# Retention in a two-layer trunk: the states of both directions in one 128-row stack

## The chip, the core and the metric

The kernel runs on one core of a Trainium2 chip. The metric is the device time of one execution in microseconds (us), as the median of several runs. The engines are TensorE (PE; its weight loads are listed apart as PEld), VectorE (DVE), ScalarE (ACT), GpSimd (POOL) and SyncE (SP, which issues the DMA transfers). Each engine works through its own list of instructions in a fixed order, and waits on semaphores for the others.

## What is computed

Two layers of a trunk over 256 context and 512 latent tokens, width 1024. Each layer projects its input to three groups of heads (a Mamba-2 SSD, a latent attention called MLA, and retention), gates each, and projects their concatenation back. The retention group has 4 heads with keys and queries of 64 and values of 128 channels, and runs a scan with a constant decay per head, once forward and once backward, in chunks of 128 tokens:

```python
def chunked_scan(q, k, v, log_a, h0):
    """h_t = exp(log_a_t) h_{t-1} + k_t v_t^T ;  y_t = q_t . h_t   (chunkwise form)"""
    ...
    y_intra = jnp.einsum('bcijgh,bcjghp->bcighp', scores[..., None] * decay, vc)
    to_end = jnp.exp(cum[:, :, -1:] - cum)
    states = jnp.einsum('bcjgn,bcjghp->bcghnp', kc, vc * to_end[..., None])
    chunk_decay = jnp.exp(cum[:, :, -1])
    ...                                   # h_in: chunk_decay * h + s, carried from chunk to chunk
    y_inter = jnp.einsum('bcign,bcghnp->bcighp', qc, h_in) * jnp.exp(cum)[..., None]

def retention_mixer(p_c, p_l, log_rate_f, log_rate_b, cos, sin, with_ctx):
    ...
    for log_rate, rev in ((log_rate_f, False), (log_rate_b, True)):
        ...
        yc, yl = directional_scan(qc, kc, vc, ..., ql, kl, vl, ..., rev)
    y_l = head_norm(ys_l[0] + ys_l[1]) ; out_l = y_l * silu(gate_l)
```

There are six chunks: 0 and 1 are context, 2 to 5 latent. The forward scan visits 0 1 2 3 4 5, the backward one 1 0 5 4 3 2. Layer 0 needs outputs for all six chunks, layer 1 only for the latent four.

## The kernel before

The tokens lie along the free dimension and channels on the 128 partitions. The program is written stage by stage, and a scheduler then sets the order of instructions on each engine from priorities and from its own idea of when things are ready; `high_priority` blocks (line 153 and others) pull work forward. So work of neighbouring stages is mixed: projections of the gate z (`zstage`, PSUM tile `pj`, names `zt`, `zy`, `yg`) run between the pieces of retention, and later ones, or products with the output weights (`po`), between those of MLA. Each 128x1024 weight tile is loaded (`wr`), cast on ScalarE (`wh`) and its remainder taken on VectorE (`wl`) before use. Projections use three products of rounded halves; retention uses float32 products, which the profile shows as two records each.

`ret` (line 730) first makes the decay tables: `Dm` for pairs of tokens inside a chunk, `ef` for queries, `te` for keys, `cd` for the carry of one chunk. It loads and rotates queries `q` and keys `kk`, two heads of 64 rows to a tile of 128 partitions. Line 781 transposes each chunk's keys on TensorE to a PSUM tile `pkt`, and line 782 copies it to `kt`. `state` (line 784) is called ten times a layer, five for each direction: VectorE multiplies `kt` by `te` to `kd`, four products with the values `rvt`, 64 columns wide, fill `prst`, and the carry (line 799, tile `rh`) adds the decayed state before. `ret_y` (line 816) is called for each pair of chunks, three times in layer 0 and twice in layer 1: scores `prs` (line 827, 64 rows each), their decayed form `mt` (tag `rmt`), decayed queries `qe` (tag `rqe`), and then line 848, for each of 4 heads and 2 chunks, one product of `rvt` with `rmt` (128 rows) and one for each direction that has an incoming state, of `rh` with `rqe` (64 rows), all into `pry`. The rest of it squares, sums (`prc`), takes the inverse root (`rs_y`, `rs_t`), spreads it (`prb`) and multiplies with the gate `rgt`.

Of the kernel before, what the change touches and what calls it, by code (L numbers as in the profile page):

```python
# [9 lines left out]
F32 = mybir.dt.float32  # L10
# [3 lines left out]
AF = mybir.ActivationFunctionType  # L14
ALU = mybir.AluOpType
# [8 lines left out]
NCH = T // 128  # L24
# [68 lines left out]
class Trunk:  # L93
# [636 lines left out]
    def ret(self, P):  # L730
        nc, l, D, ctx, lo = self.nc, self.l, self.D, self.ctx, self.lo
        pc, K = self.pc[l], self.K
        k = lambda a: K[:, a:a + 128]

        lamp = P.tile([128, 4], F32, name="lamp")
        self.act(lamp, pc[:, P_RF:P_RF + 4], AF.Exp)
        self.ts(lamp, lamp, -1.0, ALU.mult)
        lamr = P.tile([128, 8], F32, name="lamr")
        self.act(lamr, pc[:, P_RR:P_RR + 8], AF.Exp)
        self.ts(lamr, lamr, -1.0, ALU.mult)  # L740
        Dm = P.tile([128, 4, 128], F32, name="Dm")
        for h in range(4):
            self.ts(Dm[:, h], k(C_R1), lamr[:, h:h + 1], ALU.mult)
            self.stt(Dm[:, h], k(C_R2), lamr[:, 4 + h:5 + h], Dm[:, h], ALU.mult, ALU.add)
        self.act(Dm, Dm, AF.Exp)
        self.tt(Dm, Dm, k(C_OD).unsqueeze(1).to_broadcast([128, 4, 128]), ALU.mult)
        ef = P.tile([128, 2, 2, 128], F32, name="ef")
        for d in range(2):
            for p in range(2):
                self.act(ef[:, d, p], k(C_PF if d == 0 else C_PB), AF.Exp, scale=lamp[:, d * 2 + p:d * 2 + p + 1])  # L750
        cd = P.tile([128, 4], F32, name="cd")
        self.act(cd, lamp, AF.Exp, scale=128.0)
        te = P.tile([128, 2, 4], F32, name="te")
        for d in range(2):
            self.act(te[:, d], lamr[:, 4 * d:4 * d + 4], AF.Exp, scale=K[:, C_PE + d:C_PE + d + 1])
        self.ts(te, te, 0.125, ALU.mult)
        rt = P.tile([128, 2, NLAT], F32, tag="rmt", name="rt", bufs=1)
        rc, rs = rt[:, 0], rt[:, 1]
        self.load(rt, self.A["rope"][0:2].rearrange("s p t -> p s t"))

        q, kk = [], []
        for nm, src, dst, full in (("rq", D["rq"], q, ctx), ("rk", D["rk"], kk, True)):
            for t in range(2):
                u = P.tile([128, T], F32, name=f"{nm}{t}")
                a0 = 0 if full else NCTX
                self.load(u[:, a0:], src[t][:, a0:])
                w = P.tile([128, NLAT], F32, tag="rsw", name="rsw", bufs=2)
                for b in range(4):
                    self.load(w[32 * b:32 * b + 32, :], src[t][32 * (b ^ 1):32 * (b ^ 1) + 32, NCTX:T])
                self.tt(u[:, NCTX:T], u[:, NCTX:T], rc, ALU.mult)  # L770
                self.tt(w, w, rs, ALU.mult)
                self.tt(u[:, NCTX:T], u[:, NCTX:T], w, ALU.add)
                dst.append(u)
        v = P.tile([128, NCH, 512], F32, name="rvt")
        self.load(v, D["rv"])

        kt = P.tile([128, NCH, 256], F32, name="kt")
        for c in range(NCH):
            p = self.ps("py", "pkt", 2)
            for t in range(2):  # L780
                nc.tensor.transpose(p[:, t * 128:(t + 1) * 128], kk[t][:, c * 128:(c + 1) * 128], self.ident)
            self.copy(kt[:, c], p[:, 0:256])

        def state(c, d, h):
            p = self.ps("ps", "prst", 2)
            kd = P.tile([128, 4, 64], F32, tag="kd", name="kd", bufs=2)
            self.tt(kd, kt[:, c].rearrange("p (h e) -> p h e", e=64), te[:, d].unsqueeze(2).to_broadcast([128, 4, 64]),
                    ALU.mult)
            for hd in range(4):
                pr, s = divmod(hd, 2)  # L790
                self.mm(p[64 * s:64 * s + 64, pr * 128:(pr + 1) * 128], kd[:, hd, :],
                        v[:, c, hd * 128:(hd + 1) * 128])
            hn = P.tile([128, 2, 128], F32, tag=f"rh{d}", name="rh", bufs=5 if d else 3)
            pv = p[:, 0:256].rearrange("p (a e) -> p a e", e=128)
            if h is None:
                self.copy(hn, pv)
            else:
                for pr in range(2):
                    self.stt(hn[:, pr], h[:, pr], cd[:, d * 2 + pr:d * 2 + pr + 1], pv[:, pr], ALU.mult, ALU.add)
            return hn  # L800

        hs = ({}, {})
        h = None
        for c in (1, 0, 5, 4, 3, 2):
            hs[1][c] = h
            if c != 2:
                h = state(c, 1, h)
        h = None
        for c in range(NCH):
            hs[0][c] = h  # L810
            if c != NCH - 1:
                h = state(c, 0, h)
            if c % 2 == 1 and c - 1 in self.chunks:
                self.ret_y(P, c - 1, q, kk, v, Dm, ef, hs)

    def ret_y(self, P, c0, q, kk, v, Dm, ef, hs):

        nc, D = self.nc, self.D
        cs = slice(c0 * 128, (c0 + 2) * 128)
        v3 = lambda t: t.rearrange("p (a c i) -> p a c i", a=2, c=2)  # L820
        ps = [self.ps("ps", "prs", 2) for _ in range(2)]
        for h in range(4):
            pr, s = divmod(h, 2)
            r = slice(64 * s, 64 * s + 64)
            for cc in range(2):
                c1 = slice((c0 + cc) * 128, (c0 + cc + 1) * 128)
                self.mm(v3(ps[s])[:, pr, cc], kk[pr][r, c1], q[pr][r, c1])
        mt = P.tile([128, 2, 2, 2, 128], F32, tag="rmt", name="rmt", bufs=1)
        for s in range(2):
            self.tt(mt[:, s], v3(ps[s]), Dm.rearrange("p (a s) i -> p a s i", s=2)[:, :, s].unsqueeze(2)  # L830
                    .to_broadcast([128, 2, 2, 128]), ALU.mult)
        qe = P.tile([128, 2, 2, 2, 128], F32, tag="rqe", name="rqe", bufs=1)
        for d in range(2):
            for pr in range(2):
                self.tt(qe[:, d, pr], q[pr][:, cs].rearrange("p (c i) -> p c i", i=128),
                        ef[:, d, pr].unsqueeze(1).to_broadcast([128, 2, 128]), ALU.mult)
        py = [self.ps("py", "pry", 2) for _ in range(2)]
        for h in range(4):
            pr, s = divmod(h, 2)
            r = slice(64 * s, 64 * s + 64)  # L840
            for cc in range(2):
                c = c0 + cc
                ops = [(v[:, c, h * 128:(h + 1) * 128], mt[:, s, pr, cc])]
                for d in range(2):
                    if hs[d][c] is not None:
                        ops.append((hs[d][c][r, pr, :], qe[r, d, pr, cc]))
                for i, (a, b) in enumerate(ops):
                    self.mm(v3(py[s])[:, pr, cc], a, b, i == 0, i == len(ops) - 1)

        sq = P.tile([128, 2, 512], F32, tag="rmt", name="rsq", bufs=1)  # L850
        gt = P.tile([128, 2, 2, 256], F32, tag="rgt", name="rgt", bufs=1)
        pcl = self.ps("pb", "prc", 1)
        for s in range(2):
            self.act(sq[:, s], py[s], AF.Square)
            for j in range(4):
                self.mm(pcl[:, s * 4 + j:s * 4 + j + 1], sq[:, s, j * 128:(j + 1) * 128], self.ones[:, 0:1])
            for pr in range(2):
                self.load(gt[:, s, pr], D["rg"][pr * 2 + s][:, cs])
            gf = gt[:, s].rearrange("p a i -> p (a i)")
            self.tt(gf, py[s], gf, ALU.mult)  # L860
        var = P.tile([128, 8], F32, tag="rvar", name="rvar", bufs=2)
        self.ts(var, pcl[:, 0:8], 4.0 / 128, ALU.mult, 4.0 * LN_EPS, ALU.add)
        rstd = self.rsqrt(P, var, 8)
        for s in range(2):
            pb = self.ps("pb", "prb", 1)
            for j in range(4):
                self.mm(pb[:, j * 128:(j + 1) * 128], rstd[:, s * 4 + j:s * 4 + j + 1].to_broadcast([128, 128]),
                        self.ident)
            gf = gt[:, s].rearrange("p a i -> p (a i)")
            self.tt(gf, gf, pb, ALU.mult)  # L870
            for pr in range(2):
                self.load(D["m"][4 + pr * 2 + s][:, cs], gt[:, s, pr])
# [478 lines left out]
```

## Time and profile before

| what | value |
|---|---|
| three runs, us | 1536.39, 1538.78, 1549.31 (median 1538.78) |
| the profiled execution | 1534.29 us, span 1532.5 us |
| mean granted TensorE clock | 0.979 |
| TensorE, VectorE, ScalarE, GpSimd busy | 96%, 71%, 46%, 3% of the span |
| retention of layer 0, of layer 1 | about 407 to 475 us and 1183 to 1242 us after the start |

The span runs from the first to the last instruction. Busy time is the time in which an engine works on at least one instruction; a TensorE product overlaps with the next one, so the starts of products tell what each occupies better than their durations. The chain of waits goes back from the last instruction through whatever released each step; its pieces do not overlap and add up to time. A clock of 1.00 is 2.4 GHz, 0.50 is 1.2 GHz.

### The profile page before, as it was taken

To read this page: it belongs to the slowest core of one execution; us is meant where nothing else is said; L and a number is where in the kernel's file an instruction comes from. 1 tells how busy PE (TensorE), PEld (TensorE's weight loads), DVE (VectorE), ACT (ScalarE), POOL (GpSimd) and SP (SyncE) were. 2 spreads that over 40 slices of the span, in tenths; PEclk is the share of its full clock that TensorE was granted. 3 is DMA by queue.
4 is the path that set the end of the run, shared out by engine and by line. 5 is a ranking of instruction groups with operands and counts; after the bars stand their busy time and mean duration, and the time that the engine had idled before them with its cause. 6 is when DMAs were issued, how large, how long until landed. Compare 5 with 4: busy or idle time off the path is not lost. (4 is left out here: it accounts for less than half of the span.)

```text
span 1532.5 us, 24217 instructions
## 1 busy us (share of the span) xinstructions
PE 1465.7 (96%) x9044; PEld 1181.1 (77%) x9044; DVE 1085.8 (71%) x2117; ACT 709.3 (46%) x1414; POOL 48.5 (3%) x43
## 2 busy tenths in 40 slices
PE   6999999999999998999999899999999999999995
PEld 4787789778878777777788778788778777767785
DVE  3599995974544566777645978997785456888867
ACT  2356654762211434477622434565463134457743
POOL 0000000000000000000003140000000000000010
PEclk9999999999998999999999899999999999999998
DMA  8335653667614845543343233343357266544253
GB/s 330 128 112 168 196 168 115 179 203 232 206 63 131 270 150 157 165 123 126 104 143 113 99 140 106 117 138 118 99 175 250 70 193 216 144 153 122 85 178 110
DMA packets 114190, 233.52 MB, mean 152 GB/s; under 512 B 14028, under 2 KB 45644, under 8 KB 113816
## 3 DMA queue, kind: packets, MB, share of 16 engines
q1 hardware_dynamic: 114072, 231.97, 47.7%
q8 instruction: 71, 1.16, 0.3%
q14 instruction: 47, 0.39, 0.1%
HBM read 181.73 MB, written 50.20 MB: 151 GB/s over the span
## 5 line engine op out<-in xcount | busy, mean ns | idle before, releaser
L105 PE MATMUL pj<-hh,wh 128*128 128x512 f32 (+2 forms) x984 | 357.4, 364 | 2.0 <-ACT hh L119 1.6
L105 PE MATMUL pj<-hh,wl 128*128 128x512 f32 (+1 forms) x984 | 356.2, 362 | 0.0
L105 PE MATMUL pj<-hl,wh 128*128 128x512 f32 (+1 forms) x984 | 352.1, 358 | 0.0
L126 ACT CAST wh<-wr 128x1024 fp32r<-128x1024 f32 (+1 forms) x132 | 137.1, 1040 | 235.2 <-PE pj L105 100.8
L108 DVE TENSOR_TENSOR wl<-wr,wh 128x1024 fp32r<-128x1024 f32 (+1 forms) x132 | 163.5, 1239 | 81.4 <-ACT wh L126 73.2
L105 PEld LDWEIGHTS pj<-hh,wh 128*128 128x128 f32 (+1 forms) x984 | 187.1, 190 | 38.2 <-issue 13.6
L105 PEld LDWEIGHTS pj<-hh,wl 128*128 128x128 f32 x984 | 187.0, 190 | 34.3 <-issue 12.1
L105 PEld LDWEIGHTS pj<-hl,wh 128*128 128x128 f32 x984 | 187.5, 190 | 32.2 <-issue 9.5
L111 DVE SCALAR_TENSOR_TENSOR cv<-xpad,cw,cv 128x772 f32<-128x772 f32 (+1 forms) x96 | 92.0, 992 | 0.3
L119 ACT ACTIVATE pe<-psc 128x512 f32<-128x512 f32 (+1 forms) x112 | 63.7, 569 | 57.1 <-PE psc L105 52.4
L108 DVE TENSOR_TENSOR pel<-pe,peh 128x512 fp32r<-128x512 f32 (+1 forms) x112 | 70.9, 645 | 24.8 <-ACT peh L119 23.8
L1013 DVE TENSOR_REDUCE nm<-pmx 128x1 f32<-128x768 f32 (+1 forms) x80 | 67.7, 846 | 11.5 <-PE pmx L105 10.5
L105 PE MATMUL po<-sh,wh 128*128 128x512 f32 (+1 forms) x192 | 71.2, 374 | 4.1 <-ACT sh L119 2.0
L105 PE MATMUL po<-sl,wh 128*128 128x512 f32 (+1 forms) x192 | 70.4, 369 | 0.4 <-DVE sl L111 0.4
L105 PE MATMUL po<-sh,wl 128*128 128x512 f32 (+1 forms) x192 | 70.5, 368 | 0.0
L119 ACT ACTIVATE ce<-cf 64x512 f32<-64x512 f32 (+1 forms) x80 | 46.9, 586 | 43.9 <-DMA cf<-cum 43.1
L119 ACT ACTIVATE tm<-sf,dt 128x128 f32<-128x128 f32 x160 | 53.0, 392 | 30.3 <-DVE sf L108 28.5
L119 ACT ACTIVATE peh<-psc 128x512 fp32r<-128x512 f32 (+1 forms) x112 | 63.6, 568 | 0.5 <-PE ppv L105 0.2
L105 PE MATMUL po<-mr,wh 128*128 128x256 f32 (+1 forms) x256 | 56.9, 309 | 3.5 <-DVE la L111 3.5
L119 ACT ACTIVATE arg<-arg,ncb 128x128 f32<-128x128 f32 x160 | 54.4, 393 | 3.0 <-DVE arg L111 2.7
L105 PE MATMUL pv<-wl,hh 128*128 128x256 f32 x192 | 53.4, 278 | 0.9 <-DVE wl L108 0.9
L105 PE MATMUL pv<-wh,hh 128*128 128x256 f32 x192 | 53.3, 278 | 0.0
(333 smaller groups left out, 3046.7 us busy)
## 6 DMA issues: line engine op xcount, KB each, us to landing
wr<-in_win SPq DMA_DIRECT2D x82, 512.0 KB, 3.6
ar<-in_wada SPq DMA_DIRECT2D x48, 512.0 KB, 5.0
wr<-in_wout SPq DMA_DIRECT2D x48, 512.0 KB, 3.7
cf<-cum SPq DMA_DIRECT2D x80, 256.0 KB, 4.4
y<-ys SPq DMA_DIRECT2D x20, 256.0 KB, 2.5
xs<-th SPq DMA_DIRECT2D x16, 256.0 KB, 5.0
x<-in_xT SPq DMA_DIRECT2D x8, 384.0 KB, 9.2
rv<-stv SPq DMA_DIRECT2D x24, 128.0 KB, 3.8
```

The source lines that it names most:

```text
L105: return self.nc.tensor.matmul(out, lhsT=lhsT, rhs=rhs, start=start, stop=stop, **k)
L108: return self.nc.vector.tensor_tensor(out, a, b, op=op)
L111: return self.nc.vector.scalar_tensor_tensor(out, in0=a, scalar=s, in1=b, op0=op0, op1=op1)
L119: return self.nc.scalar.activation(out, in_, f, **k)
L126: self.nc.scalar.copy(hi, raw)
L1013: nc.vector.tensor_reduce(nm[:, i:i + 1], p1[:, 0:n], axis=AX.X, op=ALU.max, negate=True)
```

## The change

The state of a head becomes one tile of 128 partitions: the forward state on partitions 0 to 63, the backward one on 64 to 127. `hs` has one such tile for each chunk, 4 heads of 128 columns. The keys of a chunk are multiplied with both directions' decays at once, read from the transposes in PSUM, with no copy `kt`. One product per head and chunk, 128 columns wide, gives the chunk's contribution to both directions; ScalarE copies each half to the chunk that comes next in its direction, and VectorE then carries the states through, in place, head by head, for all chunks before any `ret_y`. In `ret_y` the queries are stacked in the same way (eight multiplications on 64 partitions in place of four on 128), so that one product of 128 rows takes the place of the two of 64. The missing states at both ends are zeros. The scores are written with alternating halves of the rows.

```diff
         cd = P.tile([128, 4], F32, name="cd")
-        self.act(cd, lamp, AF.Exp, scale=128.0)
+        for d in range(2):
+            self.act(cd[64 * d:64 * d + 64], lamr[64 * d:64 * d + 64, 4 * d:4 * d + 4], AF.Exp, scale=128.0)
...
-        kt = P.tile([128, NCH, 256], F32, name="kt")
-        for c in range(NCH):
-            p = self.ps("py", "pkt", 2)
+        order = ((0, 1, 2, 3, 4, 5), (1, 0, 5, 4, 3, 2))
+        nxt = [dict(zip(o, o[1:])) for o in order]
+        hs = [P.tile([128, 4, 128], F32, name=f"rh{c}") for c in range(NCH)]
+        for d in range(2):
+            if order[d][0] in self.chunks:
+                nc.gpsimd.memset(hs[order[d][0]][64 * d:64 * d + 64], 0.0)
+        tev = te.rearrange("p d h -> p h d").unsqueeze(3).to_broadcast([128, 4, 2, 64])
+        for c in (0, 1, 2, 5, 3, 4):
+            p = self.ps("ps", "prst", 2)
+            pk = self.ps("py", "pkt", 2)
             for t in range(2):
-                nc.tensor.transpose(p[:, t * 128:(t + 1) * 128], kk[t][:, c * 128:(c + 1) * 128], self.ident)
-            self.copy(kt[:, c], p[:, 0:256])
-        def state(c, d, h):
...
+                nc.tensor.transpose(pk[:, t * 128:(t + 1) * 128], kk[t][:, c * 128:(c + 1) * 128], self.ident)
+            kd = P.tile([128, 4, 2, 64], F32, tag="kd", name="kd", bufs=2)
+            self.tt(kd, pk[:, 0:256].rearrange("p (h e) -> p h e", e=64).unsqueeze(2).to_broadcast([128, 4, 2, 64]), tev,
                     ALU.mult)
-            for hd in range(4):
-                pr, s = divmod(hd, 2)
-                self.mm(p[64 * s:64 * s + 64, pr * 128:(pr + 1) * 128], kd[:, hd, :],
-                        v[:, c, hd * 128:(hd + 1) * 128])
...
+            for h in range(4):
+                self.mm(p[:, h * 128:(h + 1) * 128], kd[:, h].rearrange("p d e -> p (d e)"),
+                        v[:, c, h * 128:(h + 1) * 128])
+            for d in range(2):
+                if c in nxt[d]:
+                    r = slice(64 * d, 64 * d + 64)
+                    self.copy(hs[nxt[d][c]][r].rearrange("p h e -> p (h e)"), p[r, :])
+        for i in range(1, NCH):
+            for d in range(2):
+                c = order[d][i]
+                if i > 1:
+                    r = slice(64 * d, 64 * d + 64)
+                    prev = hs[order[d][i - 1]]
+                    for h in range(4):
+                        self.stt(hs[c][r, h], prev[r, h], cd[r, h:h + 1], hs[c][r, h], ALU.mult, ALU.add)
...
@@ ret_y
-        for h in range(4):
-            pr, s = divmod(h, 2)
-            r = slice(64 * s, 64 * s + 64)
+        for pr in range(2):
             for cc in range(2):
                 c1 = slice((c0 + cc) * 128, (c0 + cc + 1) * 128)
-                self.mm(v3(ps[s])[:, pr, cc], kk[pr][r, c1], q[pr][r, c1])
+                for s in range(2):
+                    r = slice(64 * s, 64 * s + 64)
+                    self.mm(v3(ps[s])[:, pr, cc], kk[pr][r, c1], q[pr][r, c1])
...
-        qe = P.tile([128, 2, 2, 2, 128], F32, tag="rqe", name="rqe", bufs=1)
-        for d in range(2):
-            for pr in range(2):
-                self.tt(qe[:, d, pr], q[pr][:, cs].rearrange("p (c i) -> p c i", i=128),
-                        ef[:, d, pr].unsqueeze(1).to_broadcast([128, 2, 128]), ALU.mult)
+        qe = P.tile([128, 4, 2, 128], F32, tag="rqe", name="rqe", bufs=1)
+        for h in range(4):
+            pr, s = divmod(h, 2)
+            r = slice(64 * s, 64 * s + 64)
+            for d in range(2):
+                self.tt(qe[64 * d:64 * d + 64, h], q[pr][r, cs].rearrange("p (c i) -> p c i", i=128),
+                        ef[r, d, pr].unsqueeze(1).to_broadcast([64, 2, 128]), ALU.mult)
...
-                ops = [(v[:, c, h * 128:(h + 1) * 128], mt[:, s, pr, cc])]
-                for d in range(2):
-                    if hs[d][c] is not None:
-                        ops.append((hs[d][c][r, pr, :], qe[r, d, pr, cc]))
-                for i, (a, b) in enumerate(ops):
-                    self.mm(v3(py[s])[:, pr, cc], a, b, i == 0, i == len(ops) - 1)
+                self.mm(v3(py[s])[:, pr, cc], v[:, c, h * 128:(h + 1) * 128], mt[:, s, pr, cc], True, False)
+                self.mm(v3(py[s])[:, pr, cc], hs[c][:, h], qe[:, h, cc], False, True)
```

The scheduler's order moves with it. On TensorE, layer 1, the state products stood before in groups of four, one group for a chunk and a direction, with a few projections between them:

```order
L105 MATMUL prst_11987<-rvt_11960,kd_11988 64x128 x4
L105 MATMUL prst_11996<-rvt_11960,kd_11997 64x128 x4
L105 MATMUL pj_12279<-hh1_2_8097,wl_12276 128x512
L105 MATMUL prst_12006<-rvt_11960,kd_12007 64x128 x4
L105 MATMUL pj_12279<-hh1_3_8098,wh_12275 128x512
L105 MATMUL pj_12279<-hl1_3_8106,wh_12275 128x512
L105 MATMUL pj_12279<-hh1_3_8098,wl_12276 128x512
L105 MATMUL prst_12016<-rvt_11960,kd_12017 64x128 x4
```

Now a group serves both directions, and the transposes of the chunks after it stand between:

```order
L105 MATMUL prst_11965<-rvt_11945,kd_11969 128x128 x4
L105 MATMUL prst_11977<-rvt_11945,kd_11981 128x128 x4
L790 MATMUL pkt_11989<-K_72,rk0_11925 128x128
L790 MATMUL pkt_11989<-K_72,rk1_11935 128x128
L790 MATMUL pkt_12000<-K_72,rk0_11925 128x128
L790 MATMUL pkt_12000<-K_72,rk1_11935 128x128
L105 MATMUL pj_12241<-hh1_3_8082,wh_12237 128x512
```

There are six such groups in a layer, where there were ten. The second place is the first `ret_y` of layer 1 on TensorE. Before, the eight scores stood in one piece, followed at once by the products of line 848, one of `rmt` and two of `rqe` in turn:

```order
L105 MATMUL pj_12279<-hl1_7_8110,wh_12275 128x512
L105 MATMUL prs_12075<-rq0_11920,rk0_11940 128x128 x2
L105 MATMUL prs_12075<-rq1_11930,rk1_11950 128x128 x2
L105 MATMUL prs_12076<-rq0_11920,rk0_11940 128x128 x2
L105 MATMUL prs_12076<-rq1_11930,rk1_11950 128x128 x2
L105 MATMUL pry_12093<-rmt_12085,rvt_11960 128x128
L105 MATMUL pry_12093<-rqe_12088,rh_12052 128x128
L105 MATMUL pry_12093<-rqe_12088,rh_12033 128x128
```

Now two projections split the scores, and 28 more stand between them and `pry` (five of the tile below, and 23 of the next); the products of `pry` follow in pairs, one of `rmt` and one of `rqe`:

```order
L105 MATMUL prst_12011<-rvt_11945,kd_12015 128x128 x4
L105 MATMUL prs_12055<-rq0_11905,rk0_11925 128x128 x2
L105 MATMUL prs_12055<-rq1_11915,rk1_11935 128x128 x2
L105 MATMUL pj_12241<-hh1_5_8084,wl_12238 128x512
L105 MATMUL pj_12241<-hh1_6_8085,wh_12237 128x512
L105 MATMUL prs_12056<-rq0_11905,rk0_11925 128x128 x2
L105 MATMUL prs_12056<-rq1_11915,rk1_11935 128x128 x2
L105 MATMUL pj_12241<-hl1_6_8093,wh_12237 128x512
```

The four scores of a piece write the same tile (`prs_12055`, then `prs_12056`), the one that belongs to one half of the rows; the alternation of the source is not in the order here. The third place is VectorE in layer 1, from the last `kd` to the first `rmt`. Before, the carry of one chunk stood between them:

```order
L108 TENSOR_TENSOR kd_12066<-kt_11962,te_11914 128x256
L111 SCALAR_TENSOR_TENSOR rh_12062<-rh_12052,cd_11912,prst_12055 128x128 x2
L108 TENSOR_TENSOR kd_12170<-kt_11962,te_11914 128x256
L111 SCALAR_TENSOR_TENSOR rh_12072<-rh_12062,cd_11912,prst_12065 128x128 x2
L108 TENSOR_TENSOR rmt_12085<-prs_12075,Dm_11896 128x512
```

Now 25 of a layer's 32 carries stand there:

```order
L108 TENSOR_TENSOR kd_12015<-pkt_12012,te_11899 128x512
L111 SCALAR_TENSOR_TENSOR rh5_11952<-rh0_11947,cd_11896,rh5_11952 64x128
L111 SCALAR_TENSOR_TENSOR rh3_11950<-rh2_11949,cd_11896,rh3_11950 64x128 x4
L111 SCALAR_TENSOR_TENSOR rh4_11951<-rh5_11952,cd_11896,rh4_11951 64x128 x4
L111 SCALAR_TENSOR_TENSOR rh4_11951<-rh3_11950,cd_11896,rh4_11951 64x128 x4
L111 SCALAR_TENSOR_TENSOR rh3_11950<-rh4_11951,cd_11896,rh3_11950 64x128 x4
L111 SCALAR_TENSOR_TENSOR rh5_11952<-rh4_11951,cd_11896,rh5_11952 64x128 x4
L108 TENSOR_TENSOR wl_12760<-wr_12757,wh_12759 128x1024
L111 SCALAR_TENSOR_TENSOR zt_12266<-zt_12266,pj_12241 128x512
L111 SCALAR_TENSOR_TENSOR rh2_11949<-rh3_11950,cd_11896,rh2_11949 64x128
L108 TENSOR_TENSOR yg0_11859<-zy_12269,zt_12266 128x512
L111 SCALAR_TENSOR_TENSOR rh2_11949<-rh3_11950,cd_11896,rh2_11949 64x128 x3
```

The first `rmt` follows this last row. Between the first transpose and the last `prb` of retention in layer 1, 121 products of z projections stand now, 71 before. In layer 1's attention, from its first score product to its last and the closing part behind it, 66 `po` products of 512 columns stood before and none now, and 53 of 256 columns before and 82 now.

## Rows read from the trace of the kernel before

**Rows 1.** The page: busy us (share of span) by engine.
```profile
PE 1465.7 (96%) x9044; PEld 1181.1 (77%) x9044; DVE 1085.8 (71%) x2117; ACT 709.3 (46%) x1414; POOL 48.5 (3%) x43
```
**Rows 2.** Stretches: us, PE, PEld, DVE, ACT, POOL busy (records), clock, DMA share, GB/s.
```profile
407.00:475.00 68.00, 68.00 (x441) 54.31 (x440) 32.97 (x86) 11.49 (x23) 0.31 (x1) 0.92 0.24 78
1183.00:1242.00 59.00, 58.77 (x362) 45.30 (x361) 29.01 (x77) 11.06 (x21) 0.31 (x1) 0.94 0.34 107
1355.00:1458.00 103.00, 102.17 (x479) 74.72 (x478) 84.11 (x131) 74.63 (x135) 0.00 (x0) 1.00 0.35 109
```
**Rows 3.** TensorE's waits, 1175 to 1330: us in total, times, longest.
```profile
PE pry L105 <- DVE rmt L108: 0.2, 1, 0.2
```
**Rows 4.** Chain of waits, layer 1's retention: start us, us, what, records.
```profile
1174.96 9.16 PE pj L105 x40
...
1187.41 1.02 PE prst L105 x16
1188.43 0.44 PE pj L105
1188.87 0.59 PE prst L105 x8
...
1199.51 8.52 PE pry L105 x48
1208.03 0.37 PE prst L105 x4
...
1217.65 1.08 PE prs L105 x8
...
1223.38 0.89 PE prb L105 x8
```
**Rows 5.** Timeline of TensorE, layer 1's first block: start us, us, records; the triple repeats.
```profile
1199.93 0.71 PE L105 MATMUL pry<-rqe,rh 64*128 64x128 f32 x4
...
1200.56 0.49 PE L105 MATMUL pry<-rmt,rvt 128*128 128x128 f32 x2
...
1200.98 0.71 PE L105 MATMUL pry<-rqe,rh 64*128 64x128 f32 x4
```
**Rows 6.** Timeline of TensorE, layer 0's first block: its first piece and the next work.
```profile
423.79 0.39 PE L105 MATMUL pry<-rmt,rvt 128*128 128x128 f32 x2
...
430.35 0.65 PE L105 MATMUL prst<-rvt,kd 128*64 128x128 f32 x6
```
**Rows 7.** VectorE by line and form, 380 to 1260: busy us, mean ns, idle before.
```profile
L111 DVE SCALAR_TENSOR_TENSOR tm<-sb,dt,tm 128x128 f32<-128x128 f32 x64 | 19.0, 344 | 0.8 <-ACT tm L119 0.8
L111 DVE SCALAR_TENSOR_TENSOR rh<-rh,cd,prst 128x128 f32<-128x128 f32 x32 | 9.8, 343 | 5.0 <-PE prst L105 4.9
L108 DVE TENSOR_TENSOR kd<-kt,te 128x256 f32<-128x256 f32 x20 | 8.2, 419 | 0.9 <-PE prst L105 0.6 <-issue 0.2
L111 DVE SCALAR_TENSOR_TENSOR zt<-zt,pj 128x512 f32<-128x512 f32 x12 | 8.2, 683 | 14.2 <-ACT zt L119 14.2
L108 DVE TENSOR_TENSOR rmt<-prs,Dm 128x512 f32<-128x512 f32 x10 | 6.8, 688 | 3.9 <-PE prs L105 3.8
```
**Rows 8.** The page, costliest groups: busy us, mean ns of one, idle before.
```profile
L108 DVE TENSOR_TENSOR wl<-wr,wh 128x1024 fp32r<-128x1024 f32 (+1 forms) x132 | 163.5, 1239 | 81.4 <-ACT wh L126 73.2
```
**Rows 9.** ScalarE by line and form, whole span.
```profile
L122 ACT COPY num<-ppv 64x512 f32<-64x512 f32 x16 | 9.2, 578 | 1.5 <-PE ppv L105 1.3
L122 ACT COPY kt<-pkt 128x256 f32<-128x256 f32 x12 | 4.1, 376 | 1.3 <-PE pkt L781 1.0
```
**Rows 10.** Stretches in which the clock falls in retention (columns as in rows 2).
```profile
430.00:440.00 10.00, 10.00 (x62) 8.20 (x61) 5.73 (x16) 2.42 (x4) 0.00 (x0) 0.83 0.04 9
460.00:470.00 10.00, 10.00 (x56) 8.57 (x55) 3.96 (x10) 0.60 (x1) 0.00 (x0) 0.79 0.08 28
1210.00:1220.00 10.00, 10.00 (x49) 8.00 (x47) 6.06 (x17) 1.23 (x2) 0.00 (x0) 0.83 0.26 79
```

More of the change, by code (lines that the diff above doesn't have):

```diff
@@ L775, in ret @@
         self.load(v, D["rv"])
-        kt = P.tile([128, NCH, 256], F32, name="kt")
-        for c in range(NCH):
-            p = self.ps("py", "pkt", 2)
-            for t in range(2):
-                nc.tensor.transpose(p[:, t * 128:(t + 1) * 128], kk[t][:, c * 128:(c + 1) * 128], self.ident)
-            self.copy(kt[:, c], p[:, 0:256])
-        def state(c, d, h):
-            p = self.ps("ps", "prst", 2)
-            kd = P.tile([128, 4, 64], F32, tag="kd", name="kd", bufs=2)
-            self.tt(kd, kt[:, c].rearrange("p (h e) -> p h e", e=64), te[:, d].unsqueeze(2).to_broadcast([128, 4, 64]),
-                    ALU.mult)
-            for hd in range(4):
-                pr, s = divmod(hd, 2)
-                self.mm(p[64 * s:64 * s + 64, pr * 128:(pr + 1) * 128], kd[:, hd, :],
-                        v[:, c, hd * 128:(hd + 1) * 128])
[L793 to L797, printed above, removed]
-                for pr in range(2):
-                    self.stt(hn[:, pr], h[:, pr], cd[:, d * 2 + pr:d * 2 + pr + 1], pv[:, pr], ALU.mult, ALU.add)
-            return hn
@@ L802, in ret @@
[L802 to L814, printed above, removed]
+        order = ((0, 1, 2, 3, 4, 5), (1, 0, 5, 4, 3, 2))
+        nxt = [dict(zip(o, o[1:])) for o in order]
@@ L816, in ret_y @@
+        for i in range(1, NCH):
[6 more added lines that the diff above has]
+                        self.stt(hs[c][r, h], prev[r, h], cd[r, h:h + 1], hs[c][r, h], ALU.mult, ALU.add)
+        for c in range(0, NCH, 2):
+            if c in self.chunks:
+                self.ret_y(P, c, q, kk, v, Dm, ef, hs)
     def ret_y(self, P, c0, q, kk, v, Dm, ef, hs):
@@ L831, in ret_y @@
                     .to_broadcast([128, 2, 2, 128]), ALU.mult)
-        qe = P.tile([128, 2, 2, 2, 128], F32, tag="rqe", name="rqe", bufs=1)
-        for d in range(2):
-            for pr in range(2):
-                self.tt(qe[:, d, pr], q[pr][:, cs].rearrange("p (c i) -> p c i", i=128),
-                        ef[:, d, pr].unsqueeze(1).to_broadcast([128, 2, 128]), ALU.mult)
+        qe = P.tile([128, 4, 2, 128], F32, tag="rqe", name="rqe", bufs=1)
[5 more added lines that the diff above has]
+                        ef[r, d, pr].unsqueeze(1).to_broadcast([64, 2, 128]), ALU.mult)
         py = [self.ps("py", "pry", 2) for _ in range(2)]
@@ L839, in ret_y @@
             pr, s = divmod(h, 2)
-            r = slice(64 * s, 64 * s + 64)
             for cc in range(2):
                 c = c0 + cc
-                ops = [(v[:, c, h * 128:(h + 1) * 128], mt[:, s, pr, cc])]
-                for d in range(2):
-                    if hs[d][c] is not None:
-                        ops.append((hs[d][c][r, pr, :], qe[r, d, pr, cc]))
-                for i, (a, b) in enumerate(ops):
-                    self.mm(v3(py[s])[:, pr, cc], a, b, i == 0, i == len(ops) - 1)
+                self.mm(v3(py[s])[:, pr, cc], v[:, c, h * 128:(h + 1) * 128], mt[:, s, pr, cc], True, False)
+                self.mm(v3(py[s])[:, pr, cc], hs[c][:, h], qe[:, h, cc], False, True)
         sq = P.tile([128, 2, 512], F32, tag="rmt", name="rsq", bufs=1)
```

## The prediction
> **What bounds the kernel now.** I read the page first. TensorE is busy 96% of the span, VectorE 71%, ScalarE 46%, GpSimd 3% [rows 1]. A busy TensorE is not one at its peak, so the next view is the two stretches in which layer 0 and layer 1 work on retention, 68 and 59 us long [rows 2]: TensorE is busy throughout, VectorE for 33.0 and 29.0 us. The waits agree: in 155 us around the second stretch `pry` waits for VectorE once, 0.2 us [rows 3]. So what a retention product occupies on TensorE is what it costs. Those prices come from the chain of waits of layer 1, whose pieces add up to time [rows 4], and from the timeline. A profiled float32 product is two records.
>
> **What a product occupies.** A projection product of 512 columns takes 9.16 / 40 = 0.229 us. Four float32 products of full height and width (`prb`) take 0.89, so one takes 0.222. One (head, chunk) of line 848, three products, is six records: layer 1's first block has 48 records in 8.52 us, eight such triples, 1.07 each [rows 4], and the others repeat it. Six records at 0.111 would be 0.67; the other 0.40 is lost at two changes of height, since the one product of `rvt` is 128 rows high and the two of `rh` are 64. In the timeline a full-height product in this alternation takes 0.42 from its start to the next one's and two half-height ones 0.63 [rows 5]. In layer 0's first block, where each chunk has one incoming state, a pair takes (430.35 − 423.79) / 8 = 0.82 [rows 6].
>
> **The change, part by part, on TensorE.**
> *Incoming states* (line 848). Triples become pairs of full-height products, and the order shows pairs: 2 × 0.222 = 0.445. There are 16 triples in layer 1 and 16 in layer 0, and 8 pairs of 0.82: 32 × (1.07 − 0.445) + 8 × (0.82 − 0.445) = 20.0 + 3.0 = **−23.0 us**.
> *State products.* Before, ten groups of four 64-column products per layer: 1.02 for a double group, seven of 0.59, and two halves of 0.37, 5.89 in all; the projection product behind a group takes 0.44 in place of 0.229 [rows 4], at some eight places, 1.7 us. Now six groups of four full-width ones, 6 × 0.89 = 5.34, with no change of width. 5.89 + 1.7 − 5.34 = 2.3 per layer, **−4.6 us**, layer 0 taken like layer 1.
> *Scores.* 40 products of 64 rows stay. The diff alternates the two row halves, but the order does not: layer 1's first eight are split by projections into two stretches of one half each. I count 15 separate half-height stretches in both layers against 10 before, so 5 × 0.40 = **+2.0 us**; products of two row halves that overlap I count at nothing, before and after.
> *Transposes*: the same 24, same price. Sum −25.6 us.
>
> The Trainium skill (TensorEngine Tiling (Array Packing), "Theoretical Speedup") states that a dimension of at most 64 lets independent tiles work side by side, for up to twice the speed. It speaks against this change, which gives up packed 64-column products; by it the state products would get slower. Worked out from rows alone: four packed products at half of 0.89, 40 of them against 24 full ones, are 4.45 against 5.34 per layer, +0.9 in place of −2.3, and the sum −25.6 + 6.4 = −19.2. The trace bears the packing out (0.59 for four, with the changes of width), but the changes eat it.
>
> **What is added elsewhere.**
> *VectorE.* `kd`: 20 of 0.419 become 12 of 128x512 read from PSUM, by `rmt` 0.688: 8.4 against 8.3. `rh`: 32 of 0.343 become 64 on 64 partitions. No row has that form; 128x128 takes 0.343 with an operand in PSUM and 0.344 without (`tm`) [rows 7], so I take 0.343 and bound it below by half: 22.0 against 11.0. `qe`: 20 of 128x256, the form of `kd` at 0.419, become 40 of as many columns: +8.4. Together +19.3 us; 62.0 + 19.3 = 81 us, under the 127 − 26 = 101 us that TensorE then needs. But all 32 `rh` now stand ahead of the first `rmt`. Behind the last `kd` of layer 1 stand 25 `rh`, one `wl`, `zt`, `yg` (priced as `zt`) and `rmt`: 8.6 + 1.24 + 0.68 + 0.68 + 0.69 = 11.9 us [rows 7, 8]. TensorE meanwhile has a state group (0.89), the scores (2 × 1.08) and 30 projection products (6.9), 10.0 us: `pry` waits 1.9. In layer 0: 30 `rh`, `zt`, `rmt`, 11.7, against 0.9 + 2.2 + 6.3 = 9.3 (15 projections of 512 columns, 24 of 256 at half): 2.4. **+4.3 us** where rows 3 had 0.2; the bounds are 0 (`rh` at half) and the whole 19.3.
> *ScalarE.* 12 `kt` copies and 4 like them go (16 × 0.376 = 6.0 us), 20 copies 64x512 of 0.578 come (11.6) [rows 9]; it is busy 22.6 of 127 us [rows 2], so nothing; uncovered it would be 5.6. One more `cd` activation per layer, beside the same slack. Two memsets on GpSimd, idle 97% of the span [rows 1]: nothing. No transfer is added; in SP's order layer 1's second gate loads stand behind two more z weights, in stretches whose DMA share is 0.24 and 0.34 [rows 2]: nothing.
> *Clock.* The mean granted clock of the two stretches is 0.92 and 0.94, 0.08 × 68 + 0.06 × 59 = 9.0 us [rows 2]. It falls in 430 to 440, 460 to 470 and 1210 to 1220 among others, with TensorE busy throughout [rows 10], each time behind a block of half-height and one-column products. The blocks get shorter and full-height, `prc` and `prb` stay. Bounds 0 and −9.0; I take half, **−4.5 us**.
> *Filler.* In layer 1's order the retention part takes 50 more z projections than before, so 66 w_out products of 512 columns that filled gaps in attention come earlier, and 29 more of 256 columns come in: 66 × 0.229 − 29 × 0.115 = 11.8 us of filler less. Attention's TensorE work without filler is about 86 of its 103 us and VectorE's 84 [rows 2], so gaps may open. Bounds 0 and 11.8; nearer 0, since VectorE's 84 includes the w_out work that leaves: **+2.5 us**.
>
> Sum: −25.6 + 4.3 − 4.5 + 2.5 = −23.3 us. The profiled execution took 1534.29 us, with 1.8 us outside its span of 1532.5; so 1511. The median of the runs shown is 4.5 higher, 1538.78, and I forecast the median: 1538.8 − 23.3 = **1515.5 us**.
>
> **The rivals.**
> *VectorE's added work comes through.* Its order is fixed, `rmt` stands behind the whole recurrence, and 16 small `rs_` operations alternate with the doubled `qe` ahead of the second block's products. If all 19.3 us are exposed and the clock stays, −25.6 + 19.3 = −6: 1532. For it: 81 of 101 us busy, in a fixed order. Against: TensorE's order puts z projections before each wait. 0.20.
> *The clock comes back whole and nothing waits*: −25.6 − 9.0 = −34.6, 1504. For it: every dip follows a block that changes. Against: `prc` stays. 0.17.
> *By the packing rule*: −19.2 in place of −25.6, the rest as above, 1522. 0.06.
> *Slower.* The 0.42 of a full-height `pry` product [rows 5] is its own price and not that of the change of height. Then a pair costs 0.84: 32 × (1.07 − 0.84) = 7.4 and nothing in the first block, while state products cost 48 × 0.42 − 12.2 = +8, scores +2: +2.6 on TensorE, and with VectorE's 19.3 exposed +22, 1561. It decides once a full-height product between its like costs over about 0.33. Against: `prb`, four in 0.89. 0.07.
> The forecast has the other 0.50.
>
> **How the numbers follow.** Within 1% is 1523.4 to 1554.2, what a measurement of this kernel can tell from no change. Faster: 0.50 + 0.17 + most of 0.06, less a tail of the forecast case, 0.71; within 1%: 0.22; slower: 0.07. The range reaches from 1500, just under the whole clock, to 1536, just over the VectorE case; outside it lies the slower case and tails.
>
> **What would show it.** Right: no `pry` record of 64 rows, pairs of 0.42 to 0.47; no 64-column `prst`, six groups of 0.9 per layer; 64 `rh` near 343 ns; `pry` waiting for `rmt` 1 to 3 us per layer; a clock above 0.95 in both stretches; few `po` of 512 columns in layer 1's attention. Wrong: pairs of 0.8; `rh` well under 0.3 (then no wait); TensorE idle for VectorE by 10 us or more in the retention stretches; attention of layer 1 no shorter although its filler has left.

## The result and the profile after

Four runs of the changed kernel have a median of 1525.3 us (1519.79 to 1530.18), those of before beside them 1538.6; the ratio is 0.990 [0.9868, 0.9932]. The same kernel in a second comparison, under the experiments, gave 1525.6 against 1542.7, 0.9892 [0.9867, 0.9917]. So the change saves some 16 us where 23.3 were forecast (1515.5 us). The profiled execution took 1519.79 us, 14.5 less than that of before.

The page of after, busy us and share of the span; it answers to [rows 1]:
```profile
PE 1440.9 (95%) x8916; PEld 1169.3 (77%) x8916; DVE 1107.2 (73%) x2161; ACT 716.9 (47%) x1420; POOL 46.6 (3%) x45
```
The three stretches of [rows 2] as they lie now (columns as there): retention of layer 0, of layer 1, attention of layer 1.
```profile
407.00:463.00 56.00, 55.50 (x408) 48.52 (x401) 45.21 (x111) 15.84 (x27) 0.00 (x0) 0.97 0.34 110
1174.00:1231.00 57.00, 56.76 (x345) 48.50 (x344) 43.10 (x102) 19.24 (x29) 0.31 (x1) 0.97 0.43 140
1346.00:1443.00 97.00, 92.97 (x442) 66.07 (x441) 75.41 (x120) 72.18 (x134) 0.00 (x0) 1.00 0.28 84
```
Layer 0's retention is 12 us shorter, layer 1's only 2, because it now holds the 50 z projections that the prediction counted (11.5 us). Attention is 6 us shorter, with the 66 long w_out products gone that it had before (15.1 us) and 29 short ones come in (3.3 us): 11.8 us of TensorE less bought 6, and TensorE, busy 102.2 of 103 us then, is busy 93.0 of 97. The chain of waits through layer 1's retention, which answers to [rows 4]:
```profile
1178.78 1.79 PE prst L105 x16
...
1186.23 1.08 PE prs L105 x8
...
1195.92 3.84 PE pry L105 x32
...
1202.78 0.65 PE prs L105 x8
```
The first block's eight heads and chunks take 3.84 us where they took 8.52: 0.48 a pair. A state group takes 0.9. Eight score records take 1.08 in the first block and 0.65 in the second. TensorE's timeline, against [rows 5]:
```profile
1195.92 0.49 PE L105 MATMUL pry<-rmt,rvt 128*128 128x128 f32 x2 [0.24 <-DVE rmt L108]
1196.25 0.39 PE L105 MATMUL pry<-rqe,rh 128*128 128x128 f32 x2
1196.47 0.39 PE L105 MATMUL pry<-rmt,rvt 128*128 128x128 f32 x2
```
From one product's start to the next one's are 0.22 us now, the price of `prb`, where a triple took 0.42 and 0.63. VectorE by form, 380 to 1260 us (busy, mean ns), against [rows 7], and its timeline ahead of layer 1's first `rmt`:
```profile
L111 DVE SCALAR_TENSOR_TENSOR rh<-rh,cd,rh 64x128 f32<-64x128 f32 x64 | 18.7, 347 | 1.9 <-ACT rh L122 1.4
L108 DVE TENSOR_TENSOR rqe<-rq,ef 64x256 f32<-64x256 f32 x32 | 13.4, 419 | 2.2 <-PE pry L105 1.6
L108 DVE TENSOR_TENSOR kd<-pkt,te 128x512 f32<-128x512 f32 x12 | 8.1, 684 | 4.4 <-PE pkt L790 4.4
```
```profile
1184.99 6.22 DVE L111 SCALAR_TENSOR_TENSOR rh<-rh,cd,rh 64x128 f32<-64x128 f32 x21
1191.31 1.23 DVE L108 TENSOR_TENSOR wl<-wr,wh 128x1024 fp32r<-128x1024 f32 x1
...
1195.18 1.29 DVE L108 TENSOR_TENSOR rmt<-prs,Dm 128x512 f32<-128x512 f32 x2
```
The three forms cost per instruction what was assumed (0.343, 0.419, 0.688). In a row, 21 carries take 6.22 us, 0.296 each: neighbours overlap, so a mean duration is too dear for a run of them. TensorE's wait for `rmt`, as in [rows 3], 1170 to 1330 us of after:
```profile
PE pry L105 <- DVE rmt L108: 0.2, 1, 0.2
```

### The profile page after: what moved, and what is told of

It is laid out like the page before. It is cut to its first block, busy times and chain, and to the rows that moved or that the text cites. A ratio compares the mean times of both kernels' runs of the same rounds, so it can differ in the third digit from the quotient of the medians.

```text
span 1518.0 us, 24021 instructions
## 1 busy us (share of the span) xinstructions
PE 1440.9 (95%) x8916; PEld 1169.3 (77%) x8916; DVE 1107.2 (73%) x2161; ACT 716.9 (47%) x1420; POOL 46.6 (3%) x45
## 5 line engine op out<-in xcount | busy, mean ns | idle before, releaser
L105 PEld LDWEIGHTS pj<-hh,wh 128*128 128x128 f32 (+1 forms) x984 | 185.5, 189 | 37.1 <-issue 12.2
```

The costliest lines, as they stand in the source:

```text
L105: return self.nc.tensor.matmul(out, lhsT=lhsT, rhs=rhs, start=start, stop=stop, **k)
```

## The experiments

Ratios are to the kernel before in the same rounds, of a median near 1543 us.

### One layer at a time
```diff
-                self.ret(P)
+                (self.ret if l == 0 else self.ret_old)(P)
```


> The change in layer 0 alone; layer 1 keeps the old retention. Theory A (layer 1 gives its gain back, because its z projections move into retention and 66 w_out products leave attention): the whole gain of the change is layer 0's, 13 to 15 us, so 1523 to 1526 us, and layer 1's attention takes 103 us as before. Rival B (both layers gain alike, about 7 us each): 1532 us.

Measured: 1524.8 us, 0.9893 [0.987, 0.9916]. The other half has `l == 1` in that line.

> The change in layer 1 alone. Theory A: 1536 to 1540 us, no change, although layer 1's products of line 848's kind take 8 us in place of 17; attention takes about 97 us with score products waiting for ScalarE. Rival B: 1532 us.

Measured: 1539.3 us, 0.9988 [0.9966, 1.001]. Layer 0's part is worth 16.5 us, as much as the whole change; layer 1's 1.9, with an interval from 5 less to 2 more. Rival B falls. Their attention, layer 0 changed and layer 1 changed:
```profile
1348.00:1451.00 103.00, 102.18 (x480) 74.72 (x479) 84.26 (x131) 74.67 (x135) 0.00 (x0) 1.00 0.37 110
```
```profile
1361.00:1459.00 98.00, 94.56 (x442) 67.13 (x440) 75.50 (x120) 72.73 (x135) 0.00 (x0) 0.98 0.29 86
```
Attention of layer 1 changes only with layer 1: it takes 103 us with the old one and 97 to 98 with the new one, as in the two main profiles.

### Height undone, number of products kept
```diff
-                self.mm(v3(py[s])[:, pr, cc], hs[c][:, h], qe[:, h, cc], False, True)
+                self.mm(v3(py[s])[:, pr, cc], hs[c][0:64, h], qe[0:64, h, cc], False, True)
```


> The changed kernel, but the product of decayed queries and states uses rows 0 to 63 alone (the backward state's part of the output is left out): as many products as in the change, every second one 64 rows high. If changes of height cost (the prediction's reading): 40 pairs of 0.82 in place of 0.48, 13.6 us more on TensorE, of which layer 1's 5.4 may be covered: 1533 to 1539 us. Rival: the number of products is what was saved, pairs stay at 0.48 and the time at 1525 us.

Measured: 1539.9 us, 0.9991 [0.9968, 1.0014], 14 us above the changed kernel. The chain of layer 1's first block:
```profile
1218.73 6.62 PE pry L105 x31
```
31 records in 6.62 us are 0.85 a pair, against 0.48; by the starts of all records `pry` takes 33.3 us in this kernel and 19.7 in the changed one. 13.6 more on TensorE became 14 in time: the gain is the change of height, and it is the same number of products that shows it. The two numbers are not one and the same, though: some of the `pry` records of this profile, the slowest of its twelve runs, stand where the clock was at half, and over all runs the clock took some 3 us more than in the changed kernel (37.3 against 34.0, see Clock below). The Trainium skill (TensorEngine Tiling (Array Packing), "Key Properties") states that a change of tiling mode drains TensorE; it gives no price, and the runs put it at about 0.35 us for there and back: 13.6 / 40 = 0.34 over all pairs, and (6.62 − 3.84) / 8 = 0.35 in layer 1's first block, at the full clock in both.

### The state products, narrow
```diff
-                self.mm(p[:, h * 128:(h + 1) * 128], kd[:, h].rearrange("p d e -> p (d e)"),
-                        v[:, c, h * 128:(h + 1) * 128])
+                for d in range(2):
+                    if c in nxt[d]:
+                        self.mm(p[64 * d:64 * d + 64, h * 128:(h + 1) * 128], kd[:, h, d],
+                                v[:, c, h * 128:(h + 1) * 128])
```


> The changed kernel with state products of 64 columns, one per direction: forward and backward in the two column halves, 40 a layer in place of 24 of 128. The prediction's sum: 2.3 us a layer more on TensorE, 4.6 in all, if the changes of width cost as before; by the rival of the packing rule, where the pairs run side by side at half of a full product's time each, 0.9 a layer less. Of layer 1's part little may reach the end: 1525 to 1530 us, or 1523 us by the rival.

Measured: 1526.4 us, 0.9886 [0.9857, 0.9916], as the changed kernel. Its chain in layer 1:
```profile
1181.02 1.02 PE prst L105 x16
...
1183.79 1.89 PE prst L105 x24
```
Eight narrow products take 1.02 us where four full ones take 0.89; over the program `prst` takes 12.0 us against 11.3. Narrow products pair up (16 records in 1.02), and 40 of them are, so paired, the work of 20 full ones against 24; that they gain nothing all the same I put down to the changes of width, which no run varies alone. The rival of the packing rule and the forecast's term both come out near zero.

### The order of the scores
```diff
-        for pr in range(2):
-            for cc in range(2):
-                for s in range(2):
+        for s in range(2):
+            for pr in range(2):
+                for cc in range(2):
```


> The changed kernel with the scores written head half by head half, as before the change. In the changed kernel four of the score blocks stand in alternation and take 0.42 us for four records or 0.65 for eight where a block of one half takes 1.08; if the alternation in the source is what does it, these become 1.08 again: some 2 us more on TensorE, 1525 to 1528 us. If the scheduler alternates them by itself, nothing changes.

Measured: 1526.2 us, 0.9902 [0.9867, 0.9937]: no difference in time, but by the starts of records the scores take 12.0 us against 10.3 in the changed kernel and 11.8 before (0.4 of the 12.0 and 0.9 of the 11.8 are blocks at the half clock). In the blocks that alternate, products of the two row halves start 7 ns apart and run side by side: a block of four records takes 0.42 in the changed kernel and 0.64 here. TensorE in 0.02 us of the changed kernel, 1202.70 to 1202.72, at the start of such a block, with two records under way:
```profile
1202.71 0.38 PE L105 MATMUL prs<-rq,rk 64*128 64x128 f32 x2
```
There the trace agrees with the Trainium skill (TensorEngine Tiling (Array Packing), "Theoretical Speedup"): up to twice the speed for 64 rows, 0.65 against 1.08 for eight records, with the changes of height inside both.

### Fillers put back into attention
The weights of the last w_out tiles (5, 6, 7) of layer 1 are held until an attention head is done, by a copy of one element into the tile that the load then fills:
```diff
+HOLD = {5: 0, 6: 2, 7: 4}
...
+            if gate is not None:
+                self.nc.gpsimd.tensor_copy(raw[0:1, 0:1], gate)
             self.load(raw[:, :n], src)
```


> The changed kernel, but in layer 1 the weights of the last three w_out tiles of the first half are loaded only behind attention heads 0, 2 and 4 (a one-element copy on GpSimd into the weight's tile holds the load), so that 72 products of 512 columns lie in attention again. Theory A: the score products' waits for ScalarE and the clock's fall near 1453 us go, 5 to 10 us less than the changed kernel, 1515 to 1520 us. Theory C (VectorE's 10 us of added work in layer 1 are what eats its gain): the gaps are VectorE's and stay, 1525 us or more.

Measured: 1528.4 us, 0.9909 [0.9886, 0.9931]; no gain. Theory A falls in this form. To see where it went I measure in layer 1 from one projection that all kernels share (the common product, some 400 us behind layer 0's last score product) to attention's first score product (`psc`): 186.5 us before, 186.2 and 186.0 in two profiles of the change, 183.0 with layer 0 alone changed, 180.1 here. Two more kernels with the new layer 1, `sc_old` and `st64`, have 188.8 and 190.3 at the time of the change, so a few us of this measure mean little. Attention starts 6 us earlier here, but then takes 107.7. The waits and the stretch around its start:
```profile
PE pmx L107 <- ACT bkh L128: 6.9, 1, 6.9
PE pmx L107 <- DVE nm L1013: 4.6, 3, 2.5
```
```profile
1330.00:1340.00 10.00, 3.02 (x6) 1.51 (x6) 8.19 (x14) 3.82 (x6) 0.00 (x0) 0.50 0.60 181
1340.00:1350.00 10.00, 6.89 (x22) 5.00 (x23) 3.94 (x7) 2.75 (x5) 0.00 (x0) 0.50 0.16 48
```
With nothing to fill it, TensorE stands idle for the first head's keys (`bkh`), the clock falls to its half level, 1.2 GHz, and the first heads are computed at that level. A gentler holding, tiles 6 and 7 behind heads 0 and 3, meant as a better version:
```diff
-HOLD = {5: 0, 6: 2, 7: 4}
+HOLD = {6: 0, 7: 3}
```

> The changed kernel with the last two w_out tiles of the first half held behind attention heads 0 and 3, 48 products of 512 columns in attention, more evenly than in the first such run. As a better version: theory F gives 2 to 5 us less than the changed kernel, if attention's free time takes 6 us of them and preparation gets 11 us of TensorE back; if the holding itself costs (a late tile, a load behind a wait), as the changed kernel or 2 us more.

Measured: 1533.5 us, 0.9933 [0.9907, 0.9958], slower than the change. It starts attention as early (180.1 us) and loses the clock in the same place for 13.7 us. The profile, at 1527.25 us, is one of the faster of the nine runs; over all of them the clock took 7 us more than in the change (means of 41.2 and 34.0, see Clock below), nearly the 8 us that it is slower.

### The z projections held back
The same copy, for the weights of z tiles 5 to 7, behind the first and the last key tile of MLA's preparation (`zg` holds one element of each key tile):
```diff
+HOLD = {5: 0, 6: 0, 7: 3}
...
+            g = HOLD.get(ti - Z_T) if l == 1 else None
-            hi, lo = self.wslot(self.A["win"][l, ti][:, :n], n)
+            hi, lo = self.wslot(self.A["win"][l, ti][:, :n], n, gate=None if g is None else self.zg[0:1, g:g + 1])
```

> The changed kernel, but in layer 1 the weights of z tiles 5, 6 and 7 are loaded only when MLA's preparation has made its first key tile (tiles 5, 6) and its last one (7), held by a one-element GpSimd copy into the weight's tile. On TensorE attention then gets the same fillers as before the change, 66 w_out products of 512 columns, and retention loses the 50 z projections that it had taken; VectorE's added work stays. Theory A2 (the order is what eats layer 1's gain: w_out products in MLA's preparation hold up its own products, and attention lacks filler): 6 to 12 us less than the changed kernel, 1513 to 1519 us. Theory C (VectorE's added 10 us per layer eat it): as the changed kernel, 1523 to 1527 us.

Measured: 1531.9 us, 0.993 [0.9904, 0.9957]. Attention has the old fillers again (103.7 us) and the time is 6 us above the changed kernel. Theory A2's forecast failed, but the run does not decide on the order alone, since the holding opened a gap of its own. Behind layer 1's retention, which now lacks the z projections, TensorE waits once for the normalised input of MLA (`nx`), and the clock stands at half there for 17.1 us in one piece:
```profile
PE pn L107 <- ACT nx L121: 11.7, 1, 11.7
1240.00:1250.00 10.00, 3.15 (x9) 0.49 (x9) 4.92 (x9) 5.00 (x6) 0.00 (x0) 0.50 0.83 287
```
The next run has nearly the old order without any holding.

### Without the carries
```diff
-                if i > 1:
+                if i > NCH:
```


> The changed kernel without the 64 carries of VectorE (each state keeps only its own chunk; the decayed sum over chunks is left out). 19 us of VectorE work go, 9.5 a layer, and the order of layer 1 falls back to nearly the old one (62 w_out products of 512 columns in attention). Theory A2: as the run with z held back, 1513 to 1519 us, all of it in layer 1, and layer 0's retention within 1 us of the changed kernel's. Theory C: 4 to 8 us less than the run with z held back, and layer 0 gains as well.

Measured: 1525.1 us, 0.9885 [0.9856, 0.9914], as the changed kernel. Attention starts 5.5 us earlier than in the change (180.7 from the common product) and takes 101.9 us, with fillers back in it: 19 us of VectorE work are worth at most a few us. Theory C falls as the main cause, and so does Theory A2: here the fillers are back in attention with no load held, and the time is the same.

### Less work for TensorE in layer 1
```diff
+            if self.l == 1 and half == 0 and t in (5, 6, 7):
+                self.mm(p[:, 0:b - a], hi[:, 0, :], mh[0][:, a:b], start=True, stop=False)
+                self.mm(p[:, 0:b - a], lo[:, 7, :], mh[7][:, a:b], start=False, stop=True)
```


> The kernel before, but in layer 1 tiles 5 to 7 of the first half of w_out compute 2 of their 24 products (the rest of these three sums is left out): 66 products of 512 columns, 15.1 us of TensorE, and those that remain lie ahead of attention, as in the change. Theory F (attention has time that only filler uses, so that what TensorE saves ahead of it comes back only in part): 5 to 8 us less than before, 0.995 to 0.997, with attention 6 to 8 us shorter. Rival G (TensorE is the bound throughout and layer 1's loss lies elsewhere): 15 us less, 0.990.

Measured: 1544.8 us, 1.002 [0.9994, 1.0046]: no gain, where theory F had 5 to 8 us and rival G 15. The same in the changed kernel:

> The changed kernel with the same 66 products left out, which stand ahead of attention here. Theory F: attention is as long as in the changed kernel, 97 to 99 us, and its start moves by what MLA's preparation was held up by w_out products: 4 to 8 us less than the changed kernel. Rival G: 15 us less. If preparation is bound by its own chain alone: no change.

Measured: 1533.6 us, 0.9945 [0.9924, 0.9965], 8 us slower than with the work in. None of the three expectations had that. Ahead of attention in this kernel, stretches and waits:
```profile
1330.00:1340.00 10.00, 1.01 (x2) 0.50 (x2) 8.71 (x13) 2.49 (x3) 0.00 (x0) 0.54 0.79 235
1340.00:1350.00 10.00, 4.44 (x9) 2.08 (x9) 7.74 (x12) 3.32 (x5) 0.00 (x0) 0.50 0.75 209
1350.00:1360.00 10.00, 8.34 (x33) 6.62 (x34) 5.54 (x8) 2.75 (x5) 0.00 (x0) 0.59 0.57 180
```
```profile
PE pmx L105 <- ACT bkh L126: 10.1, 1, 10.1
PE pmx L105 <- DVE nm L1008: 4.4, 3, 2.3
```
and the same place in the changed kernel:
```profile
1330.00:1340.00 10.00, 8.53 (x38) 6.45 (x36) 9.55 (x15) 3.31 (x5) 0.00 (x0) 1.00 0.92 273
1340.00:1350.00 10.00, 7.34 (x40) 5.31 (x41) 7.77 (x12) 3.82 (x7) 0.00 (x0) 1.00 0.73 216
```
Without the 15.1 us of w_out products TensorE has nothing to do for 10 us, the clock is at half for 27.3 us in one piece, and what comes then is done at half speed. In the kernel before, the same omission leaves attention at 106 us, with the clock at 0.95 in it:
```profile
1366.00:1472.00 106.00, 99.57 (x458) 71.70 (x458) 83.18 (x131) 73.91 (x135) 0.00 (x0) 0.95 0.38 114
```
So most of this work is not what sets layer 1's time, though TensorE is busy nearly throughout [rows 2]: it fills gaps that another chain leaves, and with it in, the clock in the same place is at 1.00. How much it would be worth without the clock can only be estimated. By the clock of every run (see Clock below) the omission cost 8 us more of clock in the kernel before and 13 in the changed one, while the medians rose by 2 and 8. Some 3 to 6 us of the 15.1 may thus have come through, no more than theory F had.

### The change once more


> The changed kernel itself once more, beside the kernel before in the same rounds, to narrow its interval: 0.987 to 0.992 of the time before. The profile of before that the prediction read had a section at the end of layer 0 that was 4 to 7 us shorter than in every run since, whether layer 0 was changed or not; if that was chance, the medians differ by more than the two profiles do.

Measured: 0.9892 [0.9867, 0.9917], above. The section at the end of layer 0, from its last score product to a projection 125.3 us behind it in the profile of before, takes 129.0 to 132.5 us in all thirteen profiles since, the two with the old layer 0 among them (129.7 and 129.1). So the profile of before was some 4 us better there, by chance as far as the profiles show, and what the two main profiles differ by, 14.5 us, is a few us short of what the change saves.

## Why the prediction was right and wrong

The direction and its cause were right, the size too large by 7 us. That it was no further off is in part luck: incoming states and state products were forecast 5 us too good, VectorE and the scores nearly 8 us too bad. By its steps:

- **Incoming states, −23.0.** Right in kind, 3 us too large. By the starts of all records `pry` fell from 39.7 us to 19.7, so by 20.0; the pairs are 0.48 and not 0.445, and 32 × 1.07 + 8 × 0.82 = 40.8 where 39.7 were measured before. That the height was paid for and not the number of products is shown by the half-height run.
- **State products, −4.6.** Too large. `prst` fell by 0.95 us (12.2 to 11.3), and the dear projections behind it were 13 at 0.349, 1.6 us above 0.229, not sixteen at 0.44: 2.5 in all. In time nothing can be measured: narrow state products in the changed kernel leave it where it was.
- **Scores, +2.0.** Wrong sign, −1.5, of which some 0.9 is not the order's but two blocks of before at the half clock. There are 15 stretches, as counted, but the overlap of products of two row halves was counted at nothing, and they overlap where the order alternates, which it does in the later blocks. I had looked at the first.
- **VectorE ahead of `rmt`, +4.3.** It came to 0.2 a layer. The carries cost 0.296 in a row, not 0.343, which is 1.2 us of the 1.9, and TensorE was a little later. That VectorE's 19 us come through, the first rival, is excluded: TensorE's waits for `rmt` are 0.2 us a layer, and taking 19 us of carries away gave nothing.
- **Clock, −4.5.** Right in the sum, wrong by layers. The two retention stretches lost 9.0 us to it before, and 0.03 × 56 + 0.03 × 57 = 3.4 now. One profile says little of the whole span: the clock was at half for 64.9 us before, and for 54.3 and 64.4 in the two profiles of the change. The clock on record for every run says more. (1 − granted clock) × span, which is half of the time spent at the half level, is on average 38.5 us over the 59 runs of before beside the experiments and 34.0 over the ten of the change, 4.5 less; and among those 59 runs one that lost 1 us more in this way was 0.85 us longer. By layers it is 30.2 with layer 0 alone changed, 8 less than before, and 40.8 with layer 1 alone, 2 more, where the forecast had 2.7 and 1.8 less. In every profile with the new layer 1 and its attention as it came, the clock falls for 6.8 us behind attention, where before it stood at 1.00. The row of the change:
```profile
1450.00:1460.00 10.00, 7.49 (x35) 6.79 (x36) 5.52 (x7) 3.65 (x4) 2.32 (x2) 0.67 0.36 106
```
- **Filler, +2.5.** This is the step that failed. Its bounds were 0 and 11.8, and the value was taken near zero with the argument that VectorE's work in attention leaves with the w_out products. Attention became 6 us shorter for 11.8 us of filler, so the term is 5.8. By layers the whole forecast was −14.6 and −8.7; measured were −16.5 and −1.9, so what is missing is layer 1's: 3.3 us of it by this term and some 4 by the clock above, as far as the two can be told apart. From the common product on, the second profile of the change and the one with only layer 0 changed differ by 4.0 us in TensorE's time, from start to start: 18.2 less (`pry` 9.4, `pj` 5.1, `pmx` 1.1, `prs` 1.0, the rest small ones) against 14.2 more, of which attention's scores `psc` have 5.1, `po` 4.6, `pdb` 1.6 and the products with the values, `ppv`, 1.4. Those products are the same in number and form, so these are waits and the lower clock. The place where the filler went is no cheaper: attention starts 186.0 to 190.3 us behind the common product in five profiles with the new layer 1 (the two of the change, `l1only`, `sc_old`, `st64`), with some 10 us of retention saved, and 186.5 and 183.0 in two with the old one.

One wait was not in the sum at all. Behind layer 0's retention TensorE waits for `nx` in all eleven profiles with the new layer 0, 1.7 to 4.6 us, and in none of the three with the old one. The line of the change, 450 to 625 us:
```profile
PE pn L105 <- ACT nx L119: 3.2, 2, 2.0
```
Together the parts as measured come to −24.0 on TensorE's retention, +0.2, +5.8, and for the clock up to −4.5, part of which is in the first number already: −18 to −22.5 where the medians give −16. The wait for `nx` would cover some of the rest; where all of it went is not shown.

The slower rival (a full-height product is dear by itself) is excluded by 0.22 from start to start. The packing rule's rival, 1522, came nearest to the time, and for another reason: its 6.4 us were to be lost in the state products, which lose nothing.

What stays open is which link of MLA's preparation sets attention's start. Where TensorE ran out of work there, its longest wait is for the first head's keys (`bkh`, 6.9 and 10.1 us), which come through memory; VectorE (96 and 78% busy in the last two stretches ahead of attention in the change) and the loads (DMA share 0.92 and 0.73) are both candidates. Neither was changed by itself.

## What to carry to other kernels

Here a change of height between neighbouring float32 products cost about a third of a microsecond for there and back (a change of width was not priced by itself). Stack operands so that neighbours have one shape, and compare the starts of products, not their durations. Ask of each stage that loses TensorE work whether TensorE's work is what ends it: leave out part of a filler once, and look at the granted clock of all runs together with the time, since the omission can cost clock and hide what it saves. Add up a gain by layers, since the same edit was worth 16.5 us in one and 2 in the other, and the clock went opposite ways in them.

## What the runs showed that was not expected

Less work made the kernel slower. With 66 products of 512 columns left out of the changed kernel (15.1 us at the full clock) it took 8 us longer: TensorE stood idle ahead of attention and the clock was at half there for 27.3 us. Over all runs the clock took 13 us more (46.9 against 34.0), which is more than the loss. And two float32 products on different row halves start 7 ns apart, so that order alone, with the same instructions, takes a block of four score records from 0.64 to 0.42 us.
